# Prelude of a hybrid attention/RWKV block: modulation weights in half rows, left half first, with the scale summed on TensorE and the shift on VectorE

## The chip, the cores and the metric

One NeuronCore of a Trainium2 chip runs one program. The metric is the device time of one execution in microseconds (us), the median of several runs. TensorE is PE in the profile, its weight loads PEld, VectorE is DVE, ScalarE is ACT, GpSimd is POOL; SyncE (SP) issues nearly all DMAs.

## The reference, cut to what matters

The program is one layer of a transformer-like block on 1024 tokens of width 1024. The change touches only how its first tensor, `u`, is made, and the first two products with it:

```
mod = silu(c) @ w_mod + b_mod                 # (1024) @ (1024 x 6144): shift1, scale1, gate1, shift2, ...
xn  = x * rsqrt(mean(x*x) + eps)              # each of the 1024 tokens
u   = xn * ln1_g * (1 + scale1) + shift1      # then token_mixer(u, ...)
proj = u @ w_in                               # blocks 24 and 25 of w_in are the low-rank (decay, a, gate) columns
```

All sums are kept at fp32 quality: `u` and every weight are split into a high part and the rest (`u_hi`, `u_lo`, `hi`, `lo`, in fp32r), and a product is three matmuls, hi·hi, lo·hi and hi·lo. Behind the prelude stand the other 24 blocks of `w_in`, the attention, the RWKV recurrence, the output products and the feed-forward part; they are the same in both kernels.

## The kernel before, in words

The prelude is written out by hand: under `tc.manual_schedule` SP, DVE and ACT execute its instructions in the order of the code, and PE's order is the code's throughout. Instructions of the later code (`load_w`: a DMA at L249, an ACT cast at L261, two DVE subtractions at L263) are put by the scheduler between those rows, and stay where they were put, since each engine executes its queue in order.

- SP loads four tiles of `x` (128 tokens x 1024, 512 KB each, L417), three row blocks of `w_mod` (128 x 1024, L421), the other four tiles of `x`, then the 13 other row blocks of the shift and scale columns of `w_mod`. A ring of seven buffers holds them: four of these are the buffers of the first four `x` tiles. Between them come blocks 24 and 25 of `w_in` (`low_load`, L425).
- ACT squares the tiles of `x` with a row sum (L431) and makes the reciprocal roots (L287, L288); DVE scales the tiles by them (`norm_x`, L437); PE transposes them in 16 groups of four (`turn`, L144), and ACT copies each group from PSUM into `xn` (L443), channel by token.
- DVE sums the modulation: for each of the 8 row blocks `ci`, `acc += w * silu(c)[ci]`, a row per partition (`mod_add`, L448 and L450), first the whole shift, then the whole scale. PE then sums `acc` over the partitions with a column of ones (`mod_sum`: matmuls with one moving column), and DVE adds the bias (`m1`, L460) and makes `A1` = (1+scale)·gain (L462). Only then is any channel's shift and scale known.
- From there 16 blocks of `u` (128 channels x 512 tokens) are made: `u_full` (DVE L476, ACT cast L477), `u_lower` (DVE L481). `low_part` multiplies each with blocks 24 and 25 of `w_in`: 6 matmuls of 512 columns for each block, 96 in all, summed in four PSUM banks `low`. `low_split` (ACT L492, DVE L493) makes the hi and lo of these two weight blocks.
- SP meanwhile loads the small weights `w2`, `g2`, `cst2` (L563 to L565) and the first weights of the main products (`raw_in16`, `raw_in12`, `raw_in20`, L249), and then weights for later modulation (`wm2_0` to `wm2_2`, L217). `raw_in` tiles share two buffers, also with `w2` and the two low-rank blocks.

The 48 matmuls that follow `low` on PE are the first of the main products (`ps_rkv`).

Of the kernel before, what the change touches and what calls it, by code (L numbers as in the profile page):

```python
# [12 lines left out]
ALU = mybir.AluOpType  # L13
# [118 lines left out]
def hybrid_block(ctx: ExitStack, tc: tile.TileContext, a, out):  # L132
# [202 lines left out]
    with ExitStack() as es:  # L335
# [67 lines left out]
        with tc.tile_pool(name="st", bufs=1) as st, tc.tile_pool(name="stp", bufs=2, space=PS) as stp, \  # L403
# [3 lines left out]
            acc = [st.tile([128, D], F32, name=f"acc{seg}") for seg in range(2)]  # L407
            junk = acc[1]
            xn = st.tile([128, KT, S], F32, name="xn")
            xs, pieces = [], {}  # L410

            def ring(tag, name, dt=F32):
                return st.tile([128, D], dt, tag=tag, name=name, bufs=3 if tag == "mw" else 4)

            def load_x(t):
                xs.append(ring("xa" if t < 4 else "xb", f"xt{t}"))
                nc.sync.dma_start(xs[t], a["x"][t * 128 : t * 128 + 128, :])  # L417

            def mod_load(seg, ci):
                w = pieces[seg, ci] = ring("mw" if len(pieces) % 7 < 3 else "xa", f"wm{seg}{ci}")  # L420
                nc.sync.dma_start(w, a["w_mod"][ci * 128 : ci * 128 + 128, seg * D : seg * D + D])  # L421

            def low_load(i):
                raw = rp.tile([128, D], F32, tag="raw", name=f"raw_in{i}")
                nc.sync.dma_start(raw, a["w_in"][i])  # L425
                if i == 24:
                    return raw, *(wp.tile([128, D], F32R, tag=f"w{h}", name=f"{h}_in{i}", bufs=2) for h in ("hi", "lo"))
                return raw, *(ring("xb", f"{h}_in{i}", F32R) for h in ("hi", "lo"))

            def square(t):  # L430
                nc.scalar.activation(junk, xs[t], AF.Square, accum_out=ssq[:, t : t + 1])  # L431

            def norm_x(half):
                hs = slice(half * 4, half * 4 + 4)
                rms_rstd(rstd[:, hs], ssq[:, hs])
# [3 lines left out]
            def turn(kt, half):  # L439
# [3 lines left out]
                nc.scalar.copy(xn[:, kt, half * NH : half * NH + NH], ps)  # L443

            def mod_add(seg, ci, cols=slice(0, D)):
                w, s_ = pieces[seg, ci][:, cols], sc[:, ci : ci + 1]
                if ci == 0:
                    ts(acc[seg][:, cols], w, s_, None, op0=ALU.mult)  # L448
                else:
                    stt(acc[seg][:, cols], w, s_, acc[seg][:, cols], op0=ALU.mult, op1=ALU.add)  # L450

            def mod_sum(seg, k0, n):
                ps = pb.tile([128, NH], F32, tag="big", name=f"mod{seg}{k0}")
                for k in range(k0, k0 + n):
                    mm(ps[:, k : k + 1], acc[seg][:, k * 128 : k * 128 + 128], ones[:, 0:1], start=True, stop=True)
                return ps

            def mod_col(seg, k0, n, ps):
                k1 = slice(seg * 8 + k0, seg * 8 + k0 + n)
                tt(m1[:, k1], ps[:, k0 : k0 + n], V("b_mod", seg * 8 + k0, n), op=ALU.add)  # L460
                if seg:
                    stt(A1[:, k0 : k0 + n], m1[:, k1], 1.0, V("ln1_g", k0, n), op0=ALU.add, op1=ALU.mult)  # L462

            def warm(n, w=None):
                for _ in range(n):
                    if w is None:
                        mm(idle[:, 0:NC1], cst[:, 0:128], cst, start=True, stop=True)
                    else:
                        mm(idle, ones, w[:, 0:NH], start=True, stop=True)
# [13 lines left out]
            def low_part(j, n):  # L483
                kt, half, cs = block(n)
                _, wh, wl = low[j]
# [4 lines left out]
            def low_split(j):  # L490
                raw, hi, lo = low[j]
                nc.scalar.copy(hi, raw)  # L492
                tt(lo, raw, f32(hi), op=ALU.subtract)  # L493

# [12 lines left out]
            idle = pb.tile([128, NH], F32, tag="big", name="idle")  # L507
# [1487 lines left out]
```

## Time and profile before

| | us |
|---|---|
| median of 3 runs | 1701.07 (1699.76 to 1704.37) |
| the profiled execution: its own time | 1704.73 |
| the profiled execution: span from the first to the last instruction | 1703.0 |
| start of the matmuls of the main products (`ps_rkv`), in that span | 76.9 |
| PE busy in the span | 1638.0 (96%) |

All rows below are of this one profiled execution, in us from the start of its span. A row of the timeline gives start, duration, engine, line, operation, output and inputs, how many, and in brackets how long the engine had been idle and what ended that. A row of the chain of waits gives start, duration and what held the end up at that time. A row of a table by windows gives, for each engine, its busy time and in brackets its instructions, then the granted TensorE clock (1.00 is full), the DMA engines' busy share and GB/s. The changed code is all in the first 77 us.

### The profile page before, as it was taken

Reading aid. Unit: us, or ns where it says so; the run is one execution under the profiler, and the core shown is the slowest. Engines: PE = TensorE matmul, PEld = TensorE weight load, DVE = VectorE, ACT = ScalarE, POOL = GpSimd, SP = SyncE. Lnnn points to the kernel's source line nnn. Section 1 sums busy time; section 2 is a strip of 40 time slices with the busy share of each in tenths; the row PEclk is TensorE's granted clock in tenths of the full one; section 3 lists DMA queues with packets and bytes.
Section 4 is the critical chain, followed back from the end, with each engine's and each line's share of the span. In section 5 each row is a group of like instructions: output and inputs, shape, how many; then the busy total and the mean of one; then the engine's idle time right before and its main releaser. Section 6 shows DMA issues by size and latency. Waiting matters only on the chain.

```text
span 1703.0 us, 26042 instructions
## 1 busy us (share of the span) xinstructions
PE 1638.0 (96%) x9772; PEld 1342.0 (79%) x9772; DVE 1220.8 (72%) x2390; ACT 808.6 (47%) x1482; POOL 143.4 (8%) x175
## 2 busy tenths in 40 slices
PE   5899999998999998999999999999999999999998
PEld 4767777786877776988878888888888888888886
DVE  5776787778676633888877634897777777787677
ACT  5453334333444554766642323654444444454455
POOL 0010101110111003123112000000000000000000
PEclk8899999999999999999999999999999999999999
DMA  8487743533342326433277611132333233484463
GB/s 328 139 314 205 192 125 97 136 106 106 91 115 75 91 81 151 141 110 107 76 265 268 246 62 63 50 105 94 123 107 103 93 117 101 163 284 153 125 215 112
DMA packets 120974, 239.85 MB, mean 141 GB/s; under 512 B 39888, under 2 KB 48336, under 8 KB 120848
## 3 DMA queue, kind: packets, MB, share of 16 engines
q1 hardware_dynamic: 112896, 220.94, 40.0%
q0 software_dynamic: 7952, 17.25, 3.8%
q8 instruction: 77, 1.26, 0.3%
q14 instruction: 49, 0.40, 0.1%
HBM read 172.59 MB, written 65.54 MB: 140 GB/s over the span
## 4 chain that ended last, share of the span: by engine, by line
PE 79%; DVE 9%; DMA 6%; ACT 2%; issue 2%; SPq 1%; DVEq 0%; ACTq 0%
PE X L140 13%; PE D L140 12%; PE Y L140 6%; PE wo L140 5%; PE br L140 5%; PE gt L140 5%; PE rk_ps L140 4%; PE qk L140 4%; PE ps_rkv L140 4%; PE W L140 3%; PE lg L140 2%; PE v L140 2%; PE ov L140 2%; PE sp L140 2%; PE tp L144 2%
## 5 line engine op out<-in xcount | busy, mean ns | idle before, releaser
L140 PE MATMUL D<-op,op 128*128 128x512 f32 x924 | 209.8, 390 | 0.0
L140 PEld LDWEIGHTS D<-op,op 128*128 128x128 f32 x924 | 173.5, 188 | 36.2 <-DVE op L1258 0.3
L140 PE MATMUL X<-T_m,S 128*128 128x512 f32 x440 | 107.3, 390 | 0.2
L140 PEld LDWEIGHTS X<-T_m,S 128*128 128x128 f32 x440 | 82.5, 188 | 18.2 <-ACT x L1534 0.6
L1257 ACT CAST op<-g 128x512 fp32r<-128x512 f32 x77 | 47.8, 621 | 74.1 <-PE D L140 48.0
L1258 DVE TENSOR_TENSOR op<-g,op 128x512 fp32r<-128x512 f32 x77 | 53.0, 689 | 41.7 <-ACT op L1257 41.7
L1494 DVE SCALAR_TENSOR_TENSOR c<-ab,vec,c 128x512 f32<-128x512 f32 x88 | 65.9, 750 | 19.5 <-ACT c L1497 17.9
L809 DVE TENSOR_TENSOR t<-E,M 128x60 f32<-128x60 f32 (+24 forms) x248 | 57.9, 233 | 30.2 <-DMA M<-sm 24.9
L1458 DVE TENSOR_TENSOR S<-ur,S 128x512 fp32r<-128x512 f32 x66 | 45.5, 691 | 35.6 <-ACT S L1454 35.5
L263 DVE TENSOR_TENSOR lo_in<-raw_in,hi_in 128x512 fp32r<-128x512 f32 x84 | 56.5, 707 | 16.1 <-PE gt L140 13.9
L1454 ACT CAST S<-ur 128x512 fp32r<-128x512 f32 x66 | 41.0, 622 | 55.6 <-DVE ur L1447 30.6
L1458 DVE TENSOR_TENSOR A<-ur,A 128x512 fp32r<-128x512 f32 x64 | 44.1, 688 | 30.9 <-ACT A L1454 30.7
L261 ACT CAST hi_in<-raw_in 128x1024 fp32r<-128x1024 f32 x42 | 44.0, 1049 | 44.3 <-PE ps_rkv L140 16.0
L140 PE MATMUL Y<-T_h,A 128*128 128x512 f32 x264 | 63.5, 390 | 0.0
L140 PE MATMUL Y<-T_h,S 128*128 128x512 f32 x264 | 63.3, 390 | 0.0
L140 PE MATMUL X<-B_b,A 128*128 128x512 f32 x252 | 60.8, 391 | 0.0
L140 PE MATMUL W<-B_f,A 128*128 128x512 f32 x252 | 60.6, 390 | 0.0
L1079 ACT ACTIVATE P<-lg,nm 128x896 f32<-128x896 f32 (+3 forms) x64 | 47.4, 743 | 22.8 <-DVE nm L1075 22.6
L811 DVE TENSOR_TENSOR E<-E,t 128x60 f32<-128x60 f32 (+24 forms) x248 | 53.8, 217 | 5.8
L140 PEld LDWEIGHTS Y<-T_h,A 128*128 128x128 f32 x264 | 49.6, 188 | 10.3
L140 PEld LDWEIGHTS Y<-T_h,S 128*128 128x128 f32 x264 | 49.6, 188 | 10.3
L1454 ACT CAST A<-ur 128x512 fp32r<-128x512 f32 x64 | 39.9, 623 | 34.2 <-PE X L140 31.5
(473 smaller groups left out, 4169.0 us busy)
## 6 DMA issues: line engine op xcount, KB each, us to landing
raw_in<-in_w_in SPq DMA_DIRECT2D x50, 512.0 KB, 3.7
wm<-in_w_mod SPq DMA_DIRECT2D x48, 512.0 KB, 7.0
ur<-in_w_up SPq DMA_DIRECT2D x44, 512.0 KB, 4.2
g<-d_g SPq DMA_DIRECT2D x35, 512.0 KB, 4.0
d_g<-gs SPq DMA_DIRECT2D x44, 256.0 KB, 2.0
d_g<-c SPq DMA_DIRECT2D x33, 256.0 KB, 4.4
d_st<-qh SPq DMA_DIRECT2D x64, 128.0 KB, 2.5
d_gate<-gs SPq DMA_DIRECT2D x32, 256.0 KB, 2.9
```

What stands on the lines that cost most here:

```text
L140: nc.tensor.matmul(o, lhsT, rhs, start=start, stop=stop, skip_group_check=more)
L144: nc.tensor.transpose(o, i, eye)
L261: nc.scalar.copy(hi, raw)
L263: nc.vector.tensor_tensor(lo[:, c : c + NH], raw[:, c : c + NH], f32(hi[:, c : c + NH]), op=ALU.subtract)
L809: tt(tv, E32[:, 0:J, s : s + 1].to_broadcast([128, J, W]), M32[:, s : s + 1, s + 1 : 32].to_broadcast([128, J, W]), op=ALU.mult)
L811: tt(E32[:, 0:J, s + 1 : 32], E32[:, 0:J, s + 1 : 32], tv, op=ALU.add)
L1079: nc.scalar.activation(e[:, 0:n], lg[:, 0:n], AF.Exp, bias=nm[:, 0:1], accum_out=nm[:, 1:2])
L1257: nc.scalar.copy(hi, src)
L1258: tt(lo, src, f32(hi), op=ALU.subtract)
L1454: nc.scalar.copy(hi, src)
L1458: tt(lo, src, f32(hi), op=ALU.subtract)
L1494: stt(c, ab[:, x + hf * NH : x + hf * NH + NH], V("conv_w", 22 * x + i), c, op0=ALU.mult, op1=ALU.add)
```

## The change

`w_mod` is loaded in pieces of half a row block (128 x 512, 256 KB), 32 of them through a ring of nine buffers: first the 16 pieces of the left half (channels 0 to 511, that is the first 8 blocks of `u`), scale and shift by turns, then the 16 of the right half. All eight tiles of `x` and block 24 of `w_in` are loaded ahead of them. PE sums the scale straight from the pieces (`mod_scale`: 4 matmuls with one moving column for each piece), DVE sums the shift (`mod_add`, half as wide). A step (`mod_step`) takes one piece of each and issues the loads of two more. The eight steps of the left half stand between the transposes of the second half of `x`; then its shift and scale are finished (`mod_cols1`), and the eight steps of the right half stand between the first 8 blocks of `u` and their 48 matmuls. The copies of the first 8 transposed groups move from ACT to DVE, the split of block 24 into the second half of the transposes, that of block 25 behind the first block of `u`.

```diff
-            for t in range(4):
-                load_x(t)
-            for m in range(3):
-                mod_load(*order[m])
-            for t in range(4, 8):
-                load_x(t)
...
+            order = [(side, ci, seg) for side in range(2) for ci in range(KT) for seg in (1, 0)]
...
+                    pieces.append(st.tile([128, NH], F32, tag="mw", name=f"wm{side}{ci}{seg}", bufs=9))
+                    c0 = seg * D + side * NH
+                    nc.sync.dma_start(pieces[-1], a["w_mod"][ci * 128 : ci * 128 + 128, c0 : c0 + NH])
...
+            def mod_scale(m, ps):
+                side, ci, _ = order[m]
+                for k in range(4):
+                    mm(ps[:, k : k + 1], pieces[m][:, k * 128 : k * 128 + 128], sc[:, ci : ci + 1],
+                       start=ci == 0 and k == 0, stop=ci == KT - 1, more=True)
...
+            def mod_step(side, ci, ps):
+                m = side * 16 + 2 * ci
+                mod_scale(m, ps)
+                mod_load()
+                mod_add(m + 1)
+                mod_load()
...
+            for kt in range(KT):
+                turn(kt, 0, nc.vector.tensor_copy)
+                if kt == 4:
+                    norm_x(1)
+            for kt in range(KT):
+                turn(kt, 1, nc.scalar.copy)
...
+                if kt == 3:
+                    low_split(raw24, *(wp.tile([128, D], F32R, tag=f"w{h}", name=f"{h}_in24", bufs=2) for h in ("hi", "lo")))
+                mod_step(0, kt, mod_ps)
+                if kt == 4:
+                    raw25 = low_load(25)
...
+            mod_cols1(0, mod_ps)
...
             u_full(0)
             for n in range(16):
+                if n == 8:
+                    warm(2)
+                    mod_cols1(1, mod_ps1)
+                    u_full(8)
-                if n < 15:
+                if n != 7 and n < 15:
                     u_full(n + 1)
                 u_lower(n)
+                if n == 0:
+                    low_split(raw25, *(st.tile([128, D], F32R, tag="xb", name=f"{h}_in25", bufs=4) for h in ("hi", "lo")))
                 low_part(0, n)
...
+                if n < 8:
+                    mod_step(1, n, mod_ps1)
+                if n == 7:
+                    w2 = rp.tile([128, S], F32, tag="raw", name="w2")
...
+                    nc.sync.dma_start(g2, a["g2"])
+                    nc.sync.dma_start(cst2, a["cst"][:, NC1:])
```

Behind the prelude every engine has the same rows in the same order in both programs, but for some 15 rows on ACT and DVE in the output products. Inside it, three places are shown. In the names, `wm150` is the piece of the right half (1), row block 5, shift (0); `wm161` that of row block 6, scale (1).

DVE, at the split of block 24 (`lo_in24`). Before, it stands behind all whole row blocks but the last, which is added in two halves (`wm17`: scale, row block 7):

```order
L450 SCALAR_TENSOR_TENSOR acc1_140<-wm15_324,sc_90,acc1_140 128x1024
L450 SCALAR_TENSOR_TENSOR acc1_140<-wm16_331,sc_90,acc1_140 128x1024
L493 TENSOR_TENSOR lo_in24_330<-raw_in24_327,hi_in24_329 128x1024
L450 SCALAR_TENSOR_TENSOR acc1_140<-wm17_343,sc_90,acc1_140 128x512 x2
L460 TENSOR_TENSOR m1_103<-mod10_369,vec_72 128x4
```

The same place of the changed kernel:

```order
L440 COPY xn_140<-tr0_7_253 128x512
L452 TENSOR_SCALAR acc_139<-wm000_163,sc_90 128x512
L454 SCALAR_TENSOR_TENSOR acc_139<-wm010_167,sc_90,acc_139 128x512
L454 SCALAR_TENSOR_TENSOR acc_139<-wm020_171,sc_90,acc_139 128x512
L497 TENSOR_TENSOR lo_in24_312<-raw_in24_159,hi_in24_311 128x1024
L454 SCALAR_TENSOR_TENSOR acc_139<-wm030_175,sc_90,acc_139 128x512
L454 SCALAR_TENSOR_TENSOR acc_139<-wm040_269,sc_90,acc_139 128x512
L454 SCALAR_TENSOR_TENSOR acc_139<-wm050_285,sc_90,acc_139 128x512
L454 SCALAR_TENSOR_TENSOR acc_139<-wm060_300,sc_90,acc_139 128x512
L454 SCALAR_TENSOR_TENSOR acc_139<-wm070_319,sc_90,acc_139 128x512
L468 TENSOR_TENSOR m1_103<-mod0_142,vec_72 128x2x4
```

It has moved ahead of five of the left half's eight shift additions, and the copies of the first transposes stand ahead of all of them.

DVE, at the passage from the left to the right half. `lo_in16` (L263) belongs to the first weight of the main products, not to the prelude. Before, it stands in the middle of the blocks of `u`, long after `m1` and `A1`:

```order
L476 TENSOR_SCALAR xn_141<-xn_141,A1_102,m1_103 128x512
L481 TENSOR_TENSOR u_lo_111<-xn_141,u_hi_110 128x512
L476 TENSOR_SCALAR xn_141<-xn_141,A1_102,m1_103 128x512
L263 TENSOR_TENSOR lo_in16_590<-raw_in16_587,hi_in16_589 128x512 x2
L481 TENSOR_TENSOR u_lo_111<-xn_141,u_hi_110 128x512
L476 TENSOR_SCALAR xn_141<-xn_141,A1_102,m1_103 128x512
```

The same place of the changed kernel:

```order
L454 SCALAR_TENSOR_TENSOR acc_139<-wm160_452,sc_90,acc_139 128x512
L486 TENSOR_TENSOR u_lo_111<-xn_140,u_hi_110 128x512
L454 SCALAR_TENSOR_TENSOR acc_139<-wm170_470,sc_90,acc_139 128x512
L263 TENSOR_TENSOR lo_in16_668<-raw_in16_665,hi_in16_667 128x512 x2
L468 TENSOR_TENSOR m1_103<-mod1_396,vec_72 128x2x4
L470 SCALAR_TENSOR_TENSOR A1_102<-m1_103,vec_72 128x4
L481 TENSOR_SCALAR xn_140<-xn_140,A1_102,m1_103 128x512 x2
L486 TENSOR_TENSOR u_lo_111<-xn_140,u_hi_110 128x512
```

The two subtractions now stand ahead of the right half's `m1` and `A1`; on ACT, the cast that feeds them has moved likewise, to just ahead of the ninth `u_hi`.

SP, from the last pieces to the first weights of the main products. Before:

```order
L421 DMA wm16_331<-in_w_mod 128x1024
L421 DMA wm17_343<-in_w_mod 128x1024
L425 DMA raw_in25_357<-in_w_in 128x1024
L563 DMA w2_385<-in_w2a2 64x512 x4
L564 DMA g2_128<-in_g2 128x512
L565 DMA cst2_120<-in_cst 128x1088
L249 DMA raw_in16_587<-in_w_in 128x1024
```

The same place of the changed kernel:

```order
L422 DMA wm161_437<-in_w_mod 128x512
L422 DMA wm160_452<-in_w_mod 128x512
L422 DMA wm171_455<-in_w_mod 128x512
L422 DMA wm170_470<-in_w_mod 128x512
L565 DMA w2_527<-in_w2a2 64x512 x4
L566 DMA g2_128<-in_g2 128x512
L567 DMA cst2_120<-in_cst 128x1088
L249 DMA raw_in16_665<-in_w_in 128x1024
```

The order of the small weights and of `raw_in16` is the same; ahead of them now stand pieces of the ring, which SP can issue only as their buffers come free: the built program has `wm170` wait for the shift sum of `wm140` (the fifth step of the right half), whose buffer it takes.

More of the change, by code (lines that the diff above doesn't have):

```diff
@@ L447, in mod_add @@
+            def mod_add(m):
+                side, ci, _ = order[m]
+                s_ = acc[:, side * NH : side * NH + NH]
                 if ci == 0:
-                    ts(acc[seg][:, cols], w, s_, None, op0=ALU.mult)
+                    ts(s_, pieces[m], sc[:, 0:1], None, op0=ALU.mult)
                 else:
[L450 to L456, printed above, removed]
@@ L465, in warm @@
+            def warm(n):
                 for _ in range(n):
[L466 to L469, printed above, removed]
+                    mm(idle[:, 0:NC1], cst[:, 0:128], cst, start=True, stop=True)
             def block(n):
```

117 lines of the change are left out of this document (40 added, 77 removed).

## The prediction

> **What bounds the kernel now.** I read the page's chain first: four fifths of it is PE, and all of the changed code lies in the first 77 us, so what matters is when PE can begin the main products, and whether anything behind them moves. The page's line, and then the chain of waits of the first 100 us (start, duration, what held the end up):
>
> ```profile
> PE 79%; DVE 9%; DMA 6%; ACT 2%; issue 2%; SPq 1%; DVEq 0%; ACTq 0%
> ```
> ```profile
> 33.38 8.58 DMA wm<-in_w_mod
> ...
> 44.83 3.56 PE mod L140 x16
> ...
> 55.33 21.57 PE low L140 x85
> 76.90 10.92 PE ps_rkv L140 x48
> ```
>
> The prelude waits for `w_mod` until 42, finishes both sums (44.83 + 3.56), and only then runs the 96 low-rank products, which end at 76.9. From there the chain is PE's. Since both programs have the same rows behind the prelude, **what the end of `low` gains or loses is the whole result**, unless a load behind it comes late.
>
> **The clock.** The granted clock by 1 us:
>
> ```profile
> 17.00:18.00 1.00, 1.00 (x7) 0.87 (x7) 0.31 (x1) 0.58 (x1) 0.00 (x0) 0.55 0.88 356
> 21.00:22.00 1.00, 0.00 (x0) 0.00 (x0) 0.00 (x0) 0.97 (x3) 0.00 (x0) 0.66 0.87 266
> 31.00:32.00 1.00, 1.00 (x6) 0.76 (x6) 0.96 (x2) 0.69 (x2) 0.00 (x0) 0.72 1.06 434
> 52.00:53.00 1.00, 1.00 (x5) 0.65 (x4) 0.01 (x1) 0.95 (x1) 0.00 (x0) 0.98 0.00 0
> 56.00:57.00 1.00, 1.00 (x4) 0.81 (x3) 1.00 (x3) 0.56 (x2) 0.00 (x0) 0.50 0.92 348
> 59.00:60.00 1.00, 1.00 (x6) 0.78 (x5) 1.00 (x2) 0.81 (x2) 0.00 (x0) 1.00 0.00 0
> ```
>
> It is 1.00 or 0.50, with fractions where it turns: up near 17.9, down at 21.3, up at 31.6, full at 52, half at 56, full by 59. Pauses of a few us drop it. Work that began at 44.83 raised it at 52, work that began at 55.33 before 59: 3.5 to 7 us bring it back.
>
> **Left half's weights, M.** I call M the start of `m1` for the left half. Rows of the `x` stage and of the prices:
>
> ```profile
> 11.26 2.74 DVE L437 TENSOR_SCALAR xt<-xt,rstd 128x1024 f32<-128x1024 f32 x4 [7.93 <-ACT rstd L288]
> 18.01 1.07 ACT L443 COPY xn<-tr 128x512 f32<-128x512 f32 x2 [0.35 <-PE tr L144]
> 20.31 1.06 ACT L431 ACTIVATE acc<-xt 128x1024 f32<-128x1024 f32 x1
> 25.36 0.21 ACT L288 ACTIVATE rstd<-rstd 128x4 f32<-128x4 f32 x1
> 10.00:15.00 5.00, 3.57 (x15) 2.31 (x13) 3.70 (x6) 1.74 (x5) 0.00 (x0) 0.95 1.00 390
> L627 DVE COPY z<-zp 128x512 f32<-128x512 f32 x8 | 5.4, 687 | 3.4 <-PE zp L140 3.4
> 15.06 3.15 PE L144 MATMUL tr<-cst,xt 128*128 128x128 f32 x14
> 28.91 5.62 PE L144 MATMUL tr<-cst,xt 128*128 128x128 f32 x29 [0.19 <-DVE xt L437]
> 34.25 1.87 PEld L140 LDWEIGHTS mod<-cst,acc 128*128 128x128 f32 x16
> L493 DVE TENSOR_TENSOR lo_in<-raw_in,hi_in 128x1024 fp32r<-128x1024 f32 x2 | 2.4, 1222 | 1.0 <-ACT hi_in L492 1.0
> L450 DVE SCALAR_TENSOR_TENSOR acc<-wm,sc,acc 128x512 f32<-128x512 f32 x2 | 1.4, 746 | 0.0
> ```
>
> The eight `x` tiles and the constants, 4.5 MB at 390 GB/s, take 11.5 us, and with 2.5 to 3.5 us until the first bytes they are in by 14 to 15. Squares and roots of four tiles take 25.57 − 20.31 = 5.3; the second set starts at 11.25, is kept to the arrival of the last tile, and is done by 16.7. DVE now copies the first transposes, a copy from PSUM being 0.69; PE's transposes at half clock (14 in 3.15, 0.225 each) set the pace as before, so the fifth copy ends near 18.7. `norm_x(1)` (2.74) then runs to 21.4, and the last three copies end at 23.7, since PE's eighth group waits for the sixth copy's bank: PE resumes at 22.1 and begins the second half at 23.0, at half clock.
>
> A step there is 4 transposes and 4 one-column matmuls. The latter cost 1.87/16 = 0.117 at full clock and 3.56/16 = 0.222 at half, so a step is 0.85 + 0.89 = 1.74 at half and some 1.1 at full. Eight of them end at 36.9 (half throughout) or 33.0 (full from 28). DVE is as late: `lo_in24` stands ahead of five shift additions and waits for ACT's copy of the fourth group (29.5) and its cast (1.04, as in the row of L261 below): it ends at 31.8 to 32.1, and five chained additions of 0.75 to 0.78 end at 35.7 to 36.0. Four matmuls with `ones` (0.5 or 0.9) follow: M = 36.2 to 37.8, **I take 37.0**. The first nine pieces, 2.4 MB, are in by 23 at the same rate and hide behind this; the rest come two by two as buffers fall free. Half rows are not in the trace of before as loads of `w_mod`; the nearest, 256 KB out of longer rows, land about as soon as the 512 KB of whole ones:
>
> ```profile
> cum<-d_lora SPq DMA_DIRECT2D x8, 256.0 KB, 3.8
> raw_in<-in_w_in SPq DMA_DIRECT2D x9, 512.0 KB, 4.4
> ```
>
> So I take their rate as unchanged. At half the rate `raw_in25`, which I expect at 38, would come at 42, and all that follows 2 to 3 us later.
>
> The Trainium skill's page "TensorE: Matmul & The Clock Gate" (Part 4) says that transposes do not count as activity for the clock gate. By that the clock stays at half until products run, and M would be 37.8 alone, 0.8 later than what I take. The trace disagrees: at 31.6 it rose in the midst of the 29 transposes of the row at 28.91, with no other work of PE ahead of it since 20.
>
> **Left half's products.** Rows of the passage from weights to products, of the pitch of a block, and of SP:
>
> ```profile
> 46.70 0.16 DVE L460 TENSOR_TENSOR m<-mod,vec 128x4 f32<-128x4 f32 x1 [1.36 <-PE mod L140]
> 48.34 0.80 PE L140 MATMUL low<-u_hi,hi_in 128*128 128x512 f32 x1
> 64.86 0.55 DVE L476 TENSOR_SCALAR xn<-xn,A,m 128x512 f32<-128x512 f32 x1
> 65.92 0.55 DVE L476 TENSOR_SCALAR xn<-xn,A,m 128x512 f32<-128x512 f32 x1
> 44.05 2.48 SPq L563 DMA_DIRECT2D w<-in_w2a  x4
> 46.57 0.59 SPq L564 DMA_DIRECT2D g<-in_g  x1
> 47.20 0.43 SPq L565 DMA_DIRECT2D cst<-in_cst  x1
> 54.24 17.87 SPq L249 DMA_DIRECT2D raw_in<-in_w_in  x3
> 57.73 1.04 ACT L261 CAST hi_in<-raw_in 128x1024 fp32r<-128x1024 f32 x1 [0.28 <-DMA raw_in<-in_w_in]
> 58.82 1.30 DVE L263 TENSOR_TENSOR lo_in<-raw_in,hi_in 128x512 fp32r<-128x512 f32 x2
> ```
>
> From `m1` to the first product: 48.34 − 46.70 = 1.64. DVE's pitch is 1.06 for a block of `u`, and 1.06 + 0.68 = 1.74 with an addition. Its first block takes longer: `u_full` twice, `u_lower`, then `lo_in25` (1.22), which waits for ACT's cast of 1.04 behind two `u_hi`, then the first addition: until M + 4.8. Four more steps (7.0) end the fifth right-half addition, of `wm140`, at M + 11.9. PE (6 products and 4 small matmuls: 1.9 a step at full clock, 3.4 at half) ends the left half at M + 17 to M + 20. The two warm-up matmuls cost nothing: PE waits there anyway.
>
> **The new wait.** `wm170`'s load needs `wm140`'s buffer. Behind it SP issues four `w2` loads (2.48), `g2` (0.59), `cst2` (0.43) and then `raw_in16`: 4.1 us with its own issue and the gaps, so at M + 16.0. It lands 57.73 − 54.24 = 3.5 later if alone, up to 4.6 behind 1.3 MB of small weights: M + 19.5 to M + 20.6. ACT's cast and DVE's two subtractions (1.04 and 1.30, 2.45 with the hand-overs) follow, and **only behind them, in DVE's queue, stands the right half's `m1`**: M + 22.0 to M + 23.1. Queued behind it are `A1` and all eight `u_full` of the right half; ACT's eight casts and PE's last 48 products wait for these. Before, the same two subtractions cost the products nothing. First right product: +1.64, at M + 24.2 (taking M + 22.6 for `m1`) = 61.2.
>
> **The sum.** The 48 products at full and at half clock:
>
> ```profile
> 69.93 6.97 PE low L140 x30
> 56.69 0.63 PE L140 MATMUL low<-u_lo,hi_in 128*128 128x512 f32 x1
> 57.11 0.63 PE L140 MATMUL low<-u_hi,hi_in 128*128 128x512 f32 x1
> ```
>
> 0.232 each at full clock (30 in 6.97), 0.425 at half. After a pause of 4 to 7 us PE starts at half; 3.1 to 7 us of that lose 1.4 to 3.2, I take 2.2. Hence 61.2 + 11.1 + 2.2 = 74.5 for the end of `low`, against 76.9: **2.4 us sooner** (with all early ends 36.2 + 22.0 + 1.6 + 11.1 + 1.4 = 72.3, with all late ends 37.8 + 23.1 + 1.6 + 11.1 + 3.2 = 76.8: 4.6 to 0.1 sooner). The loop that could have ended `low` before 70 gives most back in the stall on `raw_in16`. On the profiled execution that is 1704.7 − 2.4 = 1702.3; it ran 3.7 above the median of its runs, and from that median it is 1701.1 − 2.4 = **1698.7**. A change under 0.3% (5.1 us) can hardly be told from none here.
>
> Costed at nothing: the extra issues of SP, which waits for buffers then (without that cover 0.4 each), and POOL's `w2l`, which follows the last `u_hi` and holds only the third `raw_in` load, below.
>
> **Rivals.** (1) *The wait on `raw_in16` does not bind*, because its load is in before the left half ends. Then `m1` comes after PE's left half, at about M + 18, the pause is 2 us, and `low` ends at 37 + 18 + 1.6 + 11.1 + 1 = 68.7: 1692.9. It decides if `raw_in16` lands before M + 15.5. For it: issues vary, `w2`'s 0.62 each beside 0.43 for `cst2`. Against: it must save 4 us of a chain of which every piece has its row, and the issues can give 0.8.
>
> (2) *A load behind `low` comes late*: slower. The first weights for later modulation:
>
> ```profile
> 72.16 1.37 SPq L217 DMA_DIRECT2D wm<-in_w_mod  x3
> 80.59 1.06 ACT L261 CAST hi_in<-raw_in 128x1024 fp32r<-128x1024 f32 x1 [0.63 <-PE ps_rkv L140]
> 82.03 0.75 DVE L219 TENSOR_SCALAR acc<-wm,sc 128x1024 f32<-128x1024 f32 x1
> ```
>
> Before, three loads of `wm2` were issued from 72.16, 4.7 us ahead of the end of `low`, and the first was used 5.1 us after that end. In the changed program their buffer lies where `hi_in25` was, so they wait for the last product of `low` (the built program has them wait for that product). An issue at the end of `low`, landing 3.5 to 4.6 later, still meets its use with 0.5 to spare, and `raw_in20`, which waits for POOL's `w2l` and is cast 3.7 after the end, has about as little. If `wm2` lands later than 5.1 after `low` ends, DVE's queue is held, and the main products with it, by up to the lost lead of 4.8: 1698.7 + 4.8 = 1703.5.
>
> (3) *The split does less than it says*: the left half starts no earlier than M = 41, as when the pieces trickle. Then `low` ends at 78.5, and the time is 1702.7.
>
> **Chances.** Forecast 0.66, (1) 0.14, (2) 0.12, (3) 0.08. Faster by over 0.3%, that is under 1696.0: all of (1), and 0.08 of the forecast, where its early end meets the scatter of the runs (1.3 below their median): 0.22. Slower, over 1706.2: 0.05 of (2) and 0.04 of (3), where they meet the late end: 0.09. Within: 0.69. The range for 8 in 10 goes from rival (1), 1692.5, to just above (2), 1704.5.
>
> **What would show it.** The start of the left half's `m1` near 37, of the right half's near 60 with DVE waiting on ACT's cast and that on the DMA of `raw_in`; PE without work for 4 us or more between the halves, its clock at 0.50 behind it; the end of `low` near 74.5; the first `acc` of L219 not waiting for its DMA. A right-half `m1` before 56 would prove me wrong, and so would a main-product stage that no longer begins where `low` ends.

## The result and the profile after

The changed kernel takes 1712.26 us (median of 4 executions, 1709.46 to 1714.92), the kernel before beside it 1700.41 (median of 4, 1696.45 to 1704.37): a ratio of 1.0069, with a 95% interval of 1.0041 to 1.0098. The change costs 11.9 us; I had forecast a gain of 2.4. A later set of both gave 1712.05 (6 executions) against 1702.52 (17), ratio 1.0054, interval 1.0036 to 1.0073.

The profiled pair understates this: the changed kernel's profiled execution is its shortest (1709.46, span 1707.7), that of before its longest (1704.73, span 1703.0, above all four of its timed ones). Both kernels were therefore profiled a second time, below.

The chain of waits of the changed kernel, in its left half (start, duration, what held the end up):

```profile
24.48 1.50 PE mod L140 x8
25.98 0.96 PE tr L144 x4
...
39.20 1.50 PE mod L140 x8
40.70 0.96 PE tr L144 x4
41.66 3.22 PE mod L140 x16
```

PE alone is the chain, without a pause: 0.96 us of transposes and 1.50 of one-column matmuls in each of the eight steps, then the last step's matmuls and those with the column of ones in 3.22. The code has 4 matmuls in a step; the row counts 8. The groups of the tile `mod` (duration in ns: least, median, most) say the same for the whole program, before and after:

```profile
L140 PE MATMUL mod<-cst,acc x32: 169/296/352, 34.4 to 48.0; 128*128 128x1 f32 x32
```

```profile
L140 PE MATMUL mod<-sc,wm x128: 164/250/352, 24.3 to 68.1; 128*128 128x1 f32 x128
L140 PE MATMUL mod<-cst,acc x16: 167/301/352, 43.0 to 69.3; 128*128 128x1 f32 x16
```

The weight loads of the scale's matmuls, after:

```profile
L140 PEld LDWEIGHTS mod<-sc,wm x128: 187/333/337, 24.1 to 68.0; 128*128 128x128 f32 x128
```

Before, 16 such matmuls in the code are 32 records; after, 64 and 8 are 128 and 16, and the 128 have 128 loads. Each one-column fp32 matmul runs as two, each with its own load of 128x128 weights.

The right half, in the chain, and what follows it:

```profile
53.73 0.79 PE mod L140 x8
54.52 1.50 PE low L140 x6
...
67.52 0.79 PE mod L140 x8
68.30 0.46 PE idle L140 x2
68.76 0.80 PE mod L140 x8
...
71.24 14.07 PE low L140 x48
```

PE again without a pause: 2.29 us a step at full clock. The products end at 71.24 + 14.07 = 85.3, against 76.9 before. What DVE did at these places (timeline; in brackets how long it had been idle, and for what):

```profile
33.44 1.23 DVE L497 TENSOR_TENSOR lo_in<-raw_in,hi_in 128x1024 fp32r<-128x1024 f32 x1 [7.12 <-ACT hi_in L496]
44.90 0.17 DVE L468 TENSOR_TENSOR m<-mod,vec 128x8 f32<-128x8 f32 x1 [6.42 <-PE mod L140]
67.10 1.29 DVE L263 TENSOR_TENSOR lo_in<-raw_in,hi_in 128x512 fp32r<-128x512 f32 x2 [5.89 <-ACT hi_in L261]
69.58 0.17 DVE L468 TENSOR_TENSOR m<-mod,vec 128x8 f32<-128x8 f32 x1 [1.20 <-PE mod L140]
```

SP's row for the load behind `lo_in16`:

```profile
61.47 7.33 SPq L249 DMA_DIRECT2D raw_in<-in_w_in  x2
```

The wait on `raw_in16` that I forecast is there (issued at 61.47, the first of the two; 5.89 us idle ahead of `lo_in16` at 67.10), but it is over at 68.39, 1.2 us before PE has the sums ready. DVE waits for PE in both halves.

The table by windows (busy time and instructions of PE, PEld, DVE, ACT, POOL, then the granted clock, the DMA share and GB/s):

```profile
22.50:44.90 22.40, 22.35 (x108) 22.26 (x108) 8.04 (x12) 6.92 (x10) 0.00 (x0) 0.50 0.63 200
44.90:53.20 8.30, 6.65 (x19) 5.15 (x20) 7.23 (x14) 3.32 (x5) 0.00 (x0) 0.50 0.33 102
53.20:69.60 16.40, 16.35 (x105) 14.50 (x103) 9.31 (x17) 3.53 (x5) 0.00 (x0) 1.00 0.63 194
69.60:85.30 15.70, 14.06 (x49) 11.21 (x50) 10.11 (x22) 7.15 (x12) 2.55 (x2) 0.78 0.20 65
```

PE is busy for 22.35 of 22.40 us in the left half, and its clock stays at 0.50 throughout, and on to 53.2.

### The profile page after: what moved, and what is told of

Same layout as the page of the kernel before. It is cut to its first block, busy times and chain, and to the rows that moved or that the text cites. A ratio compares the mean times of both kernels' runs of the same rounds, so it can differ in the third digit from the quotient of the medians.

```text
span 1707.7 us, 26267 instructions
## 1 busy us (share of the span) xinstructions
PE 1654.2 (97%) x9874; PEld 1361.5 (80%) x9874; DVE 1216.8 (71%) x2396; ACT 803.6 (47%) x1474; POOL 144.8 (8%) x175
## 4 chain that ended last, share of the span: by engine, by line
PE 77%; DVE 10%; DMA 6%; ACT 3%; SPq 2%; issue 2%; DVEq 0%; POOL 0%; ACTq 0%; POOLq 0%
PE X L140 13%; PE D L140 12%; PE Y L140 6%; PE wo L140 5%; PE br L140 5%; PE gt L140 4%; PE rk_ps L140 4%; PE ps_rkv L140 4%; PE W L140 3%; PE lg L140 2%; PE ov L140 2%; PE qk L140 2%; PE v L140 2%; PE low L140 2%; PE tp L144 2%
## 5 line engine op out<-in xcount | busy, mean ns | idle before, releaser
L263 DVE TENSOR_TENSOR lo_in<-raw_in,hi_in 128x512 fp32r<-128x512 f32 x84 | 56.5, 706 | 22.6 <-PE gt L140 13.8
L261 ACT CAST hi_in<-raw_in 128x1024 fp32r<-128x1024 f32 x42 | 43.9, 1047 | 50.7 <-PE ps_rkv L140 16.2
```

Source lines behind the costliest of these rows:

```text
L263: nc.vector.tensor_tensor(lo[:, c : c + NH], raw[:, c : c + NH], f32(hi[:, c : c + NH]), op=ALU.subtract)
```

## The experiments

Ten kernels are variants of the changed one (e1 to e6, e9 to e12); e7, e8, e13 and e14 are second traces of the kernel before, of the changed one, of e12 and of e4. This table has their places in the profiled execution (us from the start of the span), and the median of their times; the kernel before, run beside each group, had medians of 1700.3 to 1702.5:

| kernel | left `m1` | right `m1` | first `ps_rkv` | median us |
|---|---|---|---|---|
| before, two traces | - | - | 76.7; 76.0 | 1700.31 (the 12 of e7) |
| changed, two traces | 44.9; 44.9 | 69.6; 74.0 | 85.1; 88.7 | 1712.05 |
| e1: 3 of 4 scale matmuls out | 35.9 | 58.7 | 73.7 | 1700.84 |
| e2: split of in16 later | 44.8 | 69.8 | 84.0 | 1709.04 |
| e3: e1 and e2 | 36.0 | 57.0 | 71.5 | 1699.04 |
| e4: both sums on VectorE, two traces | 39.1; 40.4 | 62.5; 63.8 | 77.1; 79.0 | 1706.75 (e14: 1706.99) |
| e5: idle matmuls in the left steps | 50.8 | 75.7 | 91.3 | 1716.24 |
| e6: scale on ScalarE and GpSimd, e2 | 42.9 | 68.0 | 83.2 | 1711.10 |
| e9: matmuls out in the left half only | 36.8 | 62.2 | 76.5 | 1704.57 |
| e10: scale split PE/VectorE, e2 | 39.2 | 65.2 | 79.6 | 1701.83 |
| e11: transposes first, then the steps | 45.2 | 70.2 | 85.6 | 1712.43 |
| e12: e10 with idle matmuls, two traces | 39.1; 39.4 | 61.5; 68.1 | 76.0; 82.8 | 1709.71 (e13: 1712.39) |

**Theory A**: the one-column matmuls set both halves' `m1`. **Theory B**: the half-row pieces come late. **Theory C**: my forecast's wait on `raw_in16` holds the right half.

### e1: three of four scale matmuls left out, but for the last piece of each half

```diff
             def mod_scale(m, ps):
                 side, ci, _ = order[m]
-                for k in range(4):
+                for k in range(4 if ci == KT - 1 else 1):
```

> Leaves out three of the four one-column matmuls of the scale sum for each piece except the last piece of a half (so three quarters of the scale sum are not computed); loads, order and releases of buffers stay. Theory A, the price of the one-column matmuls: each is two passes on TensorE, 0.375 us at half clock and 0.198 at full, so a left step falls from 2.46 to 0.96 + 0.375 = 1.34 us, the left half's m1 from 44.9 to 36 to 38; right steps are then bound by VectorE's 1.74, the wait for raw_in16 decides at m1 + 22, and low ends at 73.5 to 77 in place of 85.3. Theory B, the half-row pieces come late: m1 stays within 1 us of 44.9 and low ends at 84 to 85.5. Theory C, the forecast's wait for raw_in16 is what holds the right half: m1 of the left half may move, the right half's m1 follows it at a distance of 24.7 as before.

Measured: 1700.84 (ratio to before 0.9998, interval 0.9984 to 1.0012). The chain and DVE's rows:

```profile
26.05 6.16 DMA wm<-in_w_mod
32.25 3.58 PE mod L140 x16
35.86 0.18 DVE m L468
```

```profile
57.44 1.29 DVE L263 TENSOR_TENSOR lo_in<-raw_in,hi_in 128x512 fp32r<-128x512 f32 x2 [5.27 <-ACT hi_in L261]
58.65 0.16 DVE L468 TENSOR_TENSOR m<-mod,vec 128x8 f32<-128x8 f32 x1
```

The left half's `m1` comes 9.0 us sooner and the first `ps_rkv` 11.4, and the median falls by 11.2 to 11.4. Theory A's numbers hold (73.7 where 73.5 to 77 was said; `m1` a little ahead of its 36 to 38). It is not the count alone: the granted clock of e1 is 1.00 from 22 to 31 us, where the changed kernel's is 0.50. With the matmuls gone, the left half waits for its pieces (the DMA row: 6.16), and the right half's `m1` stands straight behind `lo_in16`: now the wait binds. The kernel is level with the one before, though its first `ps_rkv` stands 2 to 3 us sooner.

### e2 and e3: the split of in16 out of the way

```diff
-            nc.scalar.copy(hi, raw)
+            i = nc.scalar.copy(hi, raw)
+            if "act" in marks:
+                tc.add_manual_dep(i.ins, marks.pop("act").ins.name, NOSYNC)
...
-                    u_full(n + 1)
-                u_lower(n)
+                    i = u_full(n + 1)
+                    if n == 10:
+                        marks["act"] = i
+                i = u_lower(n)
+                if n == 10:
+                    marks["dve"] = i
```

(The subtraction on VectorE gets the same order, from `marks["dve"]`; e3 adds the edit of e1.)

> The split of in16 (cast on ScalarE, subtraction on VectorE) stands behind block 10 of the right half in place of ahead of its m1; everything is computed. Theory A (TensorE's one-column matmuls set the right half's m1): nothing moves, m1 at 69.3 to 69.7, low ends at 85.0 to 85.5, the time within 2 us of the changed kernel's. Theory C (the wait for raw_in16 sets it): m1 comes at 62 to 66, low ends at 78 to 82, the time is 3 to 7 us lower.

> Both edits: three of four one-column matmuls of the scale sum left out (three quarters of the scale sum not computed) and the split of in16 behind block 10. Theory A: with the matmuls gone the wait for raw_in16 had become the bound, so it pays now: the right half's m1 comes at the left half's + 17 to 19, at 54 to 56, and low ends at 69 to 72, 3 to 5 us ahead of the run with the matmuls left out alone and 5 to 8 ahead of the kernel before (76.9). If the wait never mattered: the same end of low as with the matmuls left out alone.

Measured: e2 1709.04 (ratio 1.0049, interval 1.0032 to 1.0067), e3 1699.04 (0.9990, 0.9975 to 1.0005). DVE in e2, then in e3:

```profile
69.82 0.17 DVE L472 TENSOR_TENSOR m<-mod,vec 128x8 f32<-128x8 f32 x1 [8.73 <-PE mod L140]
75.70 1.29 DVE L265 TENSOR_TENSOR lo_in<-raw_in,hi_in 128x512 fp32r<-128x512 f32 x2
```

```profile
57.03 0.17 DVE L472 TENSOR_TENSOR m<-mod,vec 128x8 f32<-128x8 f32 x1 [4.57 <-PE mod L140]
```

In e2 `m1` stays at 69.8, and DVE now idles 8.73 us for PE. Theory C falls: the wait is real and costs nothing while PE is later. (The first `ps_rkv` at 84.0 in place of 85.1 is the clock: the granted mean between `m1` and there is 0.88 in e2, 0.78 in the changed kernel.) The time alone would not decide it: e2's median is 3.0 to 3.2 us under the changed kernel's, where theory A said within 2 and theory C 3 to 7; the executions of the two overlap (1707.35 to 1713.87 against 1706.86 to 1714.92). The place of `m1` decides. Without the matmuls the same edit moves the first `ps_rkv` by 2.2 us, less than the 3 to 5 I expected, and its right `m1` at 57.0 is later than the 54 to 56 I gave: in the row of e3 DVE idles 4.57 us for PE even so. By the medians, 1.8 us apart, the gain of this edit can't be told from none.

### e9: which half

```diff
-                for k in range(4):
+                for k in range(1 if side == 0 and ci < KT - 1 else 4):
```

> Leaves out three of four one-column matmuls of the scale sum in the left half alone (except its last piece; that part of the scale sum is not computed); the right half has all of them. Theory A says what each half's matmuls cost: the left half's m1 comes at 35.5 to 37 as with both left out (35.9), 8 to 9 us sooner; the right half then takes 24.7 to 29 us from m1 to m1 as in the changed kernel (against 22.8 with them out), so its m1 comes at 60 to 66 and low ends at 75 to 81. If the right half's were the costly ones, low would end above 82.

Measured: 1704.57 (1.0026, 1.0012 to 1.0041).

```profile
36.76 0.17 DVE L468 TENSOR_TENSOR m<-mod,vec 128x8 f32<-128x8 f32 x1 [2.15 <-PE mod L140]
62.23 0.16 DVE L468 TENSOR_TENSOR m<-mod,vec 128x8 f32<-128x8 f32 x1
```

The left half alone gives 8.1 us of the 9.0 at its `m1`, and 8.6 of the 11.4 at the first `ps_rkv`; from `m1` to `m1` it is 25.5 with the right half's matmuls, and 22.8 without (e1). So the larger loss is the left half's, as theory A says; the right half's is 2.7 here.

### e4: the scale on VectorE too, everything else as changed

```diff
-                for k in range(4):
-                    mm(ps[:, k : k + 1], pieces[m][:, k * 128 : k * 128 + 128], sc[:, ci : ci + 1],
-                       start=ci == 0 and k == 0, stop=ci == KT - 1, more=True)
+                mod_add(m, acc_s)
```

> The scale is summed on VectorE too, in an accumulator of its own (8 ones-matmuls at the end of each half); the half-row pieces, their order and everything else stay. Theory A: TensorE's left step is 0.96, and VectorE is the bound of the left half: 16 adds of 0.72 and the 1.23 of lo_in24 from 24.3 on, then 8 ones-matmuls of 0.375 at half clock: m1 at 39.5 to 41.5. Right: VectorE's step 1.74 + 0.72 = 2.46, m1 at the left one's + 24 to 25, low ends at 79.5 to 82, between the two kernels, and the time is 3 to 6 us below the changed kernel's. Theory B (pieces late): m1 of the left half stays at 44 to 45.

Measured: 1706.75 (1.0031, 1.0020 to 1.0042).

```profile
39.14 0.17 DVE L464 TENSOR_TENSOR m<-mod,vec 128x8 f32<-128x8 f32 x1 [3.00 <-PE mod L140]
62.52 0.16 DVE L464 TENSOR_TENSOR m<-mod,vec 128x8 f32<-128x8 f32 x1
```

This is the change without its TensorE part: half rows, left half first, products of the left half while the right one loads. The left `m1` comes 5.8 us sooner with VectorE doing all 16 additions than with TensorE sharing them (4.5 in e14). Theory B falls here and in e1 as what holds the changed kernel: the pieces are there 5.8 and 9.0 us sooner, though in e1 they are then the next bound. Of the 11.9 us, the exchange of TensorE for VectorE gives back 5.3 to 5.5; the order alone is still no gain over the kernel before, but 0.2 to 0.4% slower. In the right half it takes 23.4 us from `m1` to `m1`, and the wait on `raw_in16` is among its bounds again: VectorE's last addition ends at 60.49, `lo_in16` follows at 61.30, and `m1` stands straight behind it:

```profile
59.74 0.75 DVE L450 SCALAR_TENSOR_TENSOR acc<-wm,sc,acc 128x512 f32<-128x512 f32 x1
61.30 1.29 DVE L263 TENSOR_TENSOR lo_in<-raw_in,hi_in 128x512 fp32r<-128x512 f32 x2 [0.81 <-ACT hi_in L261]
```

### e5 and e11: the clock

e5 puts two matmuls of 384 columns behind each left step, to give PE denser work; e11 runs all eight transposes of the second half first.

```diff
                 mod_step(0, kt, mod_ps)
+                warm(2)
```

> Two more matmuls of 384 columns on the constants behind each of the eight left steps; everything of the changed kernel stays. If the half clock of 22 to 53 us comes from the mix of transposes and one-column matmuls (too little work in TensorE's array), the granted clock rises to 1.0 within two of its 3.4 us windows, a left step falls from 2.46 to about 0.48 + 0.79 + 0.35 = 1.6 us, the left half's m1 comes at 37 to 40 in place of 44.9 and low ends at 77 to 80 in place of 85.3. If these matmuls do not raise the clock, a step takes about 2.46 + 0.7 = 3.1, m1 comes at 49 to 51 and low ends at 89 to 92.

```diff
                     low_split(raw24, ...
+            for kt in range(KT):
                 mod_step(0, kt, mod_ps)
```

> The left half's eight transposes-and-copies of the second half of x run first, without a one-column matmul between them; the eight steps of the scale and shift sums follow; all is computed. If transposes without gaps raise the granted clock (as they did at 31.6 in the kernel before) and the one-column matmuls keep it, the left half's m1 comes at 36 to 40 and low ends at 76 to 81. If the clock stays at half, or falls back as soon as one-column matmuls run alone: 22.5 + 7.7 + 8 x 1.5 + 3 = 45, m1 at 43.5 to 46 and low ends no sooner than 84.

Measured: e5 1716.24 (1.0089, 1.0070 to 1.0108), e11 1712.43 (1.0080, 1.0060 to 1.0100). The chain of e5 and its windows:

```profile
24.54 1.50 PE mod L140 x8
26.04 0.85 PE idle L140 x2
26.89 0.85 PE tr L144 x4
```

```profile
33.10:45.10 12.00, 12.00 (x55) 11.71 (x54) 4.89 (x6) 3.29 (x5) 0.00 (x0) 0.50 0.64 196
```

and of e11:

```profile
31.51 13.63 PE mod L140 x72
```

```profile
26.20:33.10 6.90, 4.89 (x40) 4.05 (x38) 3.13 (x5) 5.65 (x9) 0.00 (x0) 0.99 0.08 13
33.10:45.10 12.00, 12.00 (x57) 11.94 (x57) 3.75 (x5) 0.00 (x0) 0.00 (x0) 0.50 0.97 336
```

Both times the second branch came true. In e5 PE is busy for 12.00 of 12.00 us and stays at 0.50; the idle matmuls only cost their 0.74 a step. In e11 the transposes raise the clock (0.99 from 26.2 to 33.1, with PE at work for 4.89 of 6.90 us), and it falls to 0.50 within 2 us of the one-column matmuls running alone. PE had paused among the transposes before (2.01 us of 26.2 to 33.1), which may have a part in the fall; but from 33.1 on PE is busy for 12.00 of 12.00 us, and the clock does not come back. **A busy PE is not enough to raise the clock**: one-column matmuls do not. The Trainium skill's page "TensorE: Matmul & The Clock Gate" (Part 1) has the clock rise after a busy window of some 3.4 us; with busy as the profile counts it, the rows of e11 and of the changed kernel (22.35 of 22.40 us busy at 0.50) disagree. Its Part 4, by which transposes do not count as activity, is against e11's row of 26.2 to 33.1 too.

### e6: a third engine

ScalarE multiplies each piece by its column of `sc`, GpSimd adds; the split of in16 is late, as in e2.

```diff
+                nc.scalar.activation(t, pieces[m], AF.Copy, scale=sc[:, ci : ci + 1])
+                if ci:
+                    nc.gpsimd.tensor_tensor(acc_s, acc_s, t, op=ALU.add)
```

> The scale sum on neither TensorE nor VectorE: ScalarE multiplies a piece by its column of sc, GpSimd adds it to an accumulator (1.36 us for 128x512 from its rows), 8 ones-matmuls end each half; the split of in16 stands behind block 10. Theory A: left step 1.36 at most, the left half's m1 at 36 to 38.5; right bound by VectorE's 1.74, the right half's m1 at the left's + 18 to 19.5; low ends at 69 to 73, 4 to 8 us ahead of the kernel before, and the time lies 3 to 8 us under it. If GpSimd's adds slow VectorE's (or are slowed by them) to over 2.2 us a step: low ends at 76 to 80, no gain.

Measured: 1711.10 (1.0056, 1.0041 to 1.0070). GpSimd's group, and VectorE's additions without and with a GpSimd addition beside them:

```profile
L454 POOL TENSOR_TENSOR acc_s<-acc_s,wm 128x512 f32<-128x512 f32 x14 | 23.2, 1655 | 40.7 <-ACT wm L452 40.0
```

```profile
48.62 0.74 DVE L461 SCALAR_TENSOR_TENSOR acc<-wm,sc,acc 128x512 f32<-128x512 f32 x1
50.34 1.77 DVE L461 SCALAR_TENSOR_TENSOR acc<-wm,sc,acc 128x512 f32<-128x512 f32 x1
52.03 1.50 DVE L488 TENSOR_SCALAR xn<-xn,A,m 128x512 f32<-128x512 f32 x1
```

```profile
27.75 2.61 POOL L454 TENSOR_TENSOR acc_s<-acc_s,wm 128x512 f32<-128x512 f32 x2 [25.79 <-ACT wm L452]
```

The second branch by its mechanism: 0.74 becomes 1.77, and a GpSimd addition takes 1.66 on average, where the two at 27.75, with VectorE idle beside them, take 2.61 together. The left `m1` is at 42.9, the right one 25.1 later, and the first `ps_rkv` at 83.2 is later than the 76 to 80 of that branch. The Trainium skill's "GPSIMD Engine Reference" (section 1) names the SBUF interface that the two engines share, with contention for instructions with two SBUF inputs; the row at 50.34 agrees.

### e10 and e12: a version for both engines

TensorE takes one of the four column blocks of a scale piece in the left half and three in the right, VectorE the rest; the split of in16 is late. e12 adds idle matmuls in TensorE's own gaps between 28 and 41 us.

```diff
+            on_pe = (1, 3)
...
+                mod_add(m, acc_s, on_pe[side] * 128)
+                for k in range(on_pe[side]):
```

> Everything is computed: of the four column blocks of each scale piece TensorE sums one in the left half and three in the right, VectorE the others (384 columns left, 128 right), and the split of in16 stands behind block 10. Left: TensorE 0.96 + 0.375 a step, VectorE 0.72 + about 0.57, so the left half's m1 at 36 to 38. Right: TensorE 1.5 + 0.6, VectorE 1.74 + about 0.3, so m1 to m1 in 19.5 to 22.5 us; low ends at 70.5 to 75, 2 to 6 us ahead of the kernel before, and the time is 1696 to 1701. If the half clock holds on into the right half for long (as in the second look at the changed kernel, until 62.8), low ends at 75 to 78 and nothing is gained.

> The split of the scale sum between TensorE and VectorE (1 of 4 column blocks on TensorE in the left half, 3 in the right) with the split of in16 behind block 10, and with idle matmuls of 384 columns in TensorE's own gaps: 2 behind each left step from the fourth, 6 behind the last, 6 ahead of the first low product; all is computed. If the gaps of 30 to 41 us were what dropped the clock to half from 32.6 to 53.1 in the run without them, low starts at full clock, the right half runs at VectorE's 2.0 us a step, m1 to m1 takes 20 to 22.5 us in place of 26.0, low ends at 73 to 76 in place of 79.7, and the time is 1696 to 1700, 1 to 5 us under the kernel before. If the clock stays at half, they cost nothing or up to 1 us on the left half's m1, and low ends at 79 to 81.

Measured: e10 1701.83 (1.0011, 0.9997 to 1.0026), e12 1709.71 (1.0058, 1.0046 to 1.0071). e10 is level with the kernel before, not ahead: the trace has its clock at half from 32.6 to 53.1, into the right half as my second branch said, and the first `ps_rkv` at 79.6 is later than even that branch had it. e12's profiled execution did what was hoped for: full clock from 43, first `ps_rkv` at 76.0, 1703.0; its five others took 1708 to 1711. Of the versions that compute everything none beats the kernel before.

### e7, e8, e13, e14: second traces

> The kernel before, for a second profiled execution and more times: 1700 to 1703. The first one's was among its slowest times. If the part of the 11.9 us that the end of low does not explain (8.4) is only in which 3.4 us windows behind low are granted at half clock, this execution has fewer of them behind 95 us than the 31 us of the first, by about as much time as it is shorter, and its low ends at 76.5 to 77.3 again.

> The changed kernel, for a second profiled execution and more times: 1709 to 1713. low ends at 84 to 86 again. Against the second execution of the kernel before: the distance at the end of low is 7.5 to 9; if something of this kernel behind low costs the rest, the distance grows between low and the end at the same stage in both pairs; if it is chance, it grows and shrinks at other stages in this pair than in the first.

The first and the last start of this group of main products, in the order before, before again, changed, changed again:

```profile
L140 PE MATMUL ps_rkv<-u_hi,hi_in x192: 387/390/506, 76.7 to 513.8; 128*128 128x512 f32 x192
```

```profile
L140 PE MATMUL ps_rkv<-u_hi,hi_in x192: 387/389/793, 76.0 to 512.1; 128*128 128x512 f32 x192
```

```profile
L140 PE MATMUL ps_rkv<-u_hi,hi_in x192: 387/389/628, 85.1 to 520.2; 128*128 128x512 f32 x192
```

```profile
L140 PE MATMUL ps_rkv<-u_hi,hi_in x192: 387/389/797, 88.7 to 525.4; 128*128 128x512 f32 x192
```

The first pair is 8.4 us apart at the first start and 6.4 at the last; its spans differ by 4.7. The second is 12.7 and 13.3 apart, and its spans (1701.0 and 1712.9) by 11.9. So the distance is made in the prelude, and behind it moves by a few us, now down, now up. My guess for e7 was a miss: its trace has no less half clock behind 95 us than the first of the kernel before (33.7 against 31.5 us), and it is 2.0 us shorter all the same. The expectation for e8 (first `ps_rkv` at 84 to 86) was a miss: 88.7. Its windows show why:

```profile
53.20:62.80 9.60, 9.60 (x34) 8.26 (x32) 8.06 (x14) 2.47 (x4) 0.00 (x0) 0.50 0.74 230
62.80:74.00 11.20, 11.18 (x73) 9.98 (x72) 1.29 (x2) 1.05 (x1) 0.00 (x0) 1.00 0.36 132
```

The left half is the same to 0.04 us (`m1` at 44.94 and 44.90), but the half clock lasts until 62.8 in place of 53.2, and the right half's `m1` comes 4.4 us later. The same happened to e12's kernel:

> The kernel of the split with idle matmuls, for a second trace: its first profiled execution took 1703.0, its five others 1708.4 to 1711.2. If this one is a usual execution (1708 or more) and the difference is the prelude's clock: half clock for 10 us or more between 41 and 62, where the first trace had full clock from 43, low ends 4 us or more behind the first trace's 76.2, and behind low the two keep their distance within 2 us. If it lies behind low: low ends within 1 us of 76.2 and the distance grows at a later stage, at which this trace shows more half-clock windows.

> The kernel with both sums on VectorE, for a second trace: its first profiled execution took 1704.5, the median was 1706.8. No one-column matmuls run inside its halves. If the prelude's clock moves the end of low from execution to execution: low ends at another place than 77.3, by 1 us or more, and the time moves with it. If low ends within 1 us of 77.3 and the time is 1706 or more, the difference lies behind low, at the stages with other half-clock windows.

e13 took 1712.4, e14 1707.0. Two windows of e12 and of e13:

```profile
46.50:60.20 13.70, 13.70 (x83) 12.02 (x82) 10.94 (x22) 3.09 (x5) 0.00 (x0) 1.00 0.71 224
60.20:68.10 7.90, 6.21 (x27) 4.84 (x25) 6.35 (x14) 4.47 (x7) 0.00 (x0) 0.78 0.05 18
```

```profile
46.50:60.20 13.70, 13.70 (x46) 11.67 (x44) 11.27 (x23) 3.10 (x5) 0.00 (x0) 0.50 0.72 227
60.20:68.10 7.90, 7.86 (x50) 6.99 (x50) 0.00 (x0) 0.00 (x0) 0.00 (x0) 1.00 0.07 28
```

The same program, with the left `m1` at 39.1 and 39.4, PE busy for 13.70 of 13.70 us in both: 83 instructions at clock 1.00 in one, 46 at 0.50 in the other. The first `ps_rkv` comes 6.8 us later, and the end 9.3: behind it the two part by another 2.5, more than the 2 I had allowed. e14's comes 1.9 later than e4's (79.0 against 77.1), its span is 2.5 longer. In these three kernels the greater part of the difference between two executions (3.6 of 5.2, 6.8 of 9.3, 1.9 of 2.5) arises ahead of the first `ps_rkv`; in the kernel before it is 0.7 of 2.0. Why the clock was taken from one execution and not from the other, at the same work, the traces don't show.

## Why the prediction was wrong

The forecast put the end of `low` at 74.5; the two traces have 85.3 and 88.9, that is 10.8 and 14.4 later. By its steps:

- **Left half's weights, M: this is the step that failed.** "A step there is 4 transposes and 4 one-column matmuls. The latter cost 1.87/16 = 0.117 at full clock and 3.56/16 = 0.222 at half". The rows x16 that I divided were 8 matmuls of the code, recorded as two each. A step's matmuls cost 1.50 at half clock, not 0.89, and 0.79 at full, not 0.46. M is 44.9, not 37.0: 7.9 of the 10.8 (and of the 14.4). Against my value with half clock throughout, 37.8, the 36 matmuls up to `m1` explain 9 x (1.50 − 0.89) = 5.5 of 7.1, transposes of 0.96 in place of 0.85 in eight steps another 0.9 (my own row, 0.225 each, would have given 0.90), and the steps' start at 23.5 in place of 23.0 another 0.5. e1 takes most of these matmuls out and gets 35.9. The count could have been had beforehand: `mod_sum` issues 8 matmuls for its 8 columns, and the row beside it said 16.
- **The clock.** In the left half my range had both cases, full from 28 and half throughout. I let the full clock return within 3.5 to 7 us of work. Before the right half's last products it did (5.8 and 4.1 us after the first of them). Among the left half's products, with the right half's one-column matmuls between them, it stayed at 0.50 to 53.2 and 62.8, that is for 6.7 and 16.2 us after the first product at 46.55. In the left half it never came in 22 us of work. That is the later of my two cases, but not because transposes do not count, the reason weighed there: e11 shows that the transposes alone raise it and that one-column matmuls alone do not. I judged the clock by whether PE is busy; in these rows it goes by what PE is busy with.
- **Left half's products.** "6 products and 4 small matmuls: 1.9 a step at full clock, 3.4 at half": measured 2.29 at full (1.50 + 0.79), the same error. PE was through with the left half's products and the right half's sums not at M + 17 to M + 20 but at M + 24.7 and M + 29.1, and with it came the right half's `m1`, where I had M + 22.6: 2.1 and 6.5 of the loss. The further 4.4 of the second execution is its longer half clock. PE's rest between the halves was 1.7 us, not 4 or more.
- **The new wait.** It came nearly as forecast: the issue of `raw_in16` at 61.5 is M + 16.6 (forecast M + 16.0), `lo_in16` ends at M + 23.5 (forecast M + 22.0 to 23.1). But it did not bind, as PE was 1.2 us later still (e2). In e1, with PE out of the way, it does: 58.65 is M + 22.8 (forecast M + 22.0 to 23.1). So the mechanism was right for a kernel that this one is not. (The term M + 11.9 in it is 4.8 + 7.0 = 11.8.)
- **Right half's products.** From `m1` to the end of `low` I had 14.9; it is 15.7 and 14.9.
- **Behind `low`.** "What the end of `low` gains or loses is the whole result" holds within the scatter: the mean of the two traces of each kernel is 86.9 and 76.35 at the first `ps_rkv`, 10.6 apart, and the medians are 9.5 to 11.9 apart. Over all 16 traces, from 71.5 (e3) to 91.3 (e5) at the first `ps_rkv`, what follows up to the end of the span takes 1621.1 to 1628.1 us: a scatter of 7, in which my 2.4 could not have been seen. e1 is the test of the forecast without its wrong price: 35.9, 58.65 and 73.7 where I had 37.0, 59.6 and 74.5; its median is 1.0 us under that of the kernel before, a difference that its interval does not tell from none. Rival (2), the late `wm2`, did not come: DVE's first addition of it (L219) is 5.1 us behind the end of `low`, as before.
- **The rate of half rows**, taken as that of whole ones, is some tenth lower: e11's row has 336 GB/s at a DMA share of 0.97, my row of 10 to 15 us had 390 at 1.00. In the changed kernel PE covers this.
- **Rival (3)**, "the split does less than it says", had the right sign and place and the wrong cause and size: not pieces that trickle (e4), but PE. I gave it 41 for M and 0.08; what came was 44.9. No case of mine had PE as the bound of both halves, and this was the one.

What stays open is how the clock decides between e12 and e13, and with it part of why e4 and e9, whose first `ps_rkv` stands level with that of before in one trace, are 3.6 to 5 us slower in the median. The traced executions of e4, e9 and e12 were the shortest of theirs (1704.54, 1701.52, 1703.03), so their places in the table are those of a short execution and not of the median. e14 (1.9 later than e4) points to the prelude's clock; for e9 there is one trace only.

## What to carry to other kernels

Count a matmul's records against the code before dividing a row: here an fp32 matmul with one moving column cost two weight loads, 0.2 us at full clock and 0.375 at half, and each piece took four such matmuls where VectorE needed one addition of 0.74. Before moving work to an engine that has gaps, work out its pace in every loop that the work enters: in the left half PE became the only engine in the chain. And judge the clock by the kind of matmul that would run, with the measured half-clock price as the first guess wherever thin matmuls are the bulk.

## What the runs showed of the hardware

- One-column fp32 matmuls alone do not raise the clock from half while PE is busy throughout: 12.00 of 12.00 us at 0.50 in e11, right after 6.9 us at 0.99. In steps with four transposes it stayed at half as well (22.35 of 22.40 us busy, the changed kernel), and with two matmuls of 384 columns added to each step (e5).
- Mixed with products of 512 columns it may go either way at the same work: six one-column records to six products had 1.00 in e12 and 0.50 in e13 over the same 13.7 us; eight to six, in the changed kernel, had half clock until 53.2 in one execution and 62.8 in another.
- A GpSimd addition and a VectorE instruction on SBUF side by side: 0.74 becomes 1.77 for the addition with two tensor inputs, 0.54 becomes 1.50 for the one at L488 with one (e6).
